# A gated MLP after the last norm: GpSimd's passes go to VectorE, sixteen products move ahead, and down adds into y at once

## The chip, the cores and the metric

The kernel runs on one core of a Trainium2 chip. The metric is the device time of one execution in microseconds. Inputs and outputs are float32.

## The reference

One decoder layer on 512 prompt positions and on 8 sequences of 8 new positions (576 tokens together). The change touches its second half alone:

```python
def conv_ffn(hn, prev_g, w_gate, w_up, conv_w, conv_b, w_down):
    g = hn @ w_gate                     # (T, 2048) @ (2048, 5504)
    u = hn @ w_up
    gp = jnp.concatenate([prev_g.astype(g.dtype), g], axis=1)
    gc = conv_b + sum(conv_w[j] * gp[:, j:j + T] for j in range(CONV_W))
    return (jax.nn.silu(gc) * u) @ w_down, gp[:, T:]
...
    h = x + jnp.concatenate([oa.reshape(B, T, -1), ob.reshape(B, T, -1)], axis=-1) @ w_out
    f, new_g = conv_ffn(rms_norm(h, g_ffn), prev_g, w_gate, w_up, conv_w, conv_b, w_down)
    return h + f, new_rows + (new_g,)
```

## The kernel before

Everything is held transposed: features on the 128 partitions, the 576 tokens along the free dimension in two halves of 288. A float32 product is made of three reduced-precision (float32r) matmuls: each operand is split into a high part (`upper`, a cast on ScalarE, L1571) and a low part (`lower`, a subtraction, L1576), and `multiply` (L1579) runs high x high, high x low and low x high into one PSUM bank. One product of a gate tile is 8 blocks of 128 features times 3, or 24 matmuls of 128x128 by 128x288.

The stages that matter, in order:

- **w_out** (L1657, 16 steps). Each step adds a product to h, squares it on ScalarE (`square`, L1591) and sums the squares on GpSimd (L1595). The first half of h is normalised between the steps (`half0`).
- **Tile 0** (L1752 to L1814). The four weight blocks of tile 0 are multiplied with the first half of h, 4 products, two for gate and two for up. Then the second half is normalised (`norm`, L1767; `normed_h`, L1783 and L1787), and the sums and differences of the halves' blocks are made and split (`tsub`, `thigh`, `tlow`, L1784 to L1797). Then come the other 4 products, and tile 0's convolution and gating.
- **Gate and up, tiles 1 to 42** (L1887). A tile is 128 columns of w_gate and of w_up. The 2x2 block product (gate/up by two halves of the features, times two halves of the features by two halves of the tokens) is made with 7 products in place of 8 (Winograd's form of Strassen's scheme): products 1 and 2 take the blocks a11 and a12 as they are, the others take sums. `ORDER` is 1, 5, 6, 3, 7, 2, 4, and three PSUM banks hold running sums: products 1, 6, 7 and 4 go one after the other into bank "a", 5 and 3 into "b", 2 into "c". Between two products into one bank the running sum is read: ScalarE copies it (`p1s`, `p5s`, `u2s`, L1899 to L1903), or VectorE adds it to a copy. Operands are made three products ahead (`ahead`, L1872; `operand`, L1836): VectorE makes the sums (L1841 to L1850), ScalarE the high parts, and the low parts of products 7, 2 and 4 are GpSimd's, the others VectorE's. The four blocks of the next tile are loaded into 4 buffers (`wr`) as they come free; `wu` and `wl` have 4 buffers each. `conv` (L1728) is one pass on ScalarE, two on VectorE and a silu on ScalarE; `gated` (L1737) multiplies on GpSimd and stores the result to DRAM (`adr`).
- **Down** (L2035). Seven groups q of six row tiles (the last has seven), and four column groups g: 28 items of 7 products, each for two column tiles s, 126 matmuls an item. Weights are 128x768 passes. ScalarE copies products 1, 5 and 6 into snapshots, VectorE adds a snapshot to the bank, and GpSimd adds that to `ht`, which holds y (L2057 to L2065). The activations of the next q (`Acts`) are loaded from `adr`, and eleven passes of 128x864 on VectorE and seven on ScalarE make their sums and parts; they run in the item g = 3 for the most part, when the buffers of the present q come free.
- Outputs are transposed and stored (L2017).

Every load and store named here is issued by SyncE, in one queue. Each engine's instructions run in an order that the framework fixes when it builds the kernel, by a simulated schedule over the program order; buffers are reused only when their readers are done.

Of the kernel before, what the change touches and what calls it, by code (L numbers as in the profile page):

```python
# [48 lines left out]
    0, 1024, 2048, 3072, 3080, 4104, 4360, 4616, 5640, 5704)  # L49
NLATE = 5  # L50
CT = 3


@with_exitstack
def tile_hymba_step(
# [1680 lines left out]

    def gated(j, u):  # L1737

        G.tensor_mul(u[:, :TP], gc[:, :TP], u[:, :TP])
        us = u[:, TP:TP + 56].rearrange("p (b t) -> p b t", t=8)  # L1740
        G.tensor_mul(us, gc[:, TP + 2:TP + 72].rearrange("p (b t) -> p b t", t=10)[:, :, 0:8], us)
        G.tensor_mul(u[:, TP + 56:NT], gc[:, TP + 72:TP + 80], u[:, TP + 56:NT])
        S.dma_start(adr[j], u)

    def blocks(j):
# [3 lines left out]
    V.memset(gx[:, 0:2], 0.0)  # L1749
    states(0)  # L1750

    w0 = {}  # L1752
    for name, at in blocks(0).items():
        t = wload(*at)
        h = upper(t, 1024)
        w0[name] = (h, lower(t, h, 1024, G if name[1] == "2" else V))
    first = [(psum_g(), keep) for keep in (wb.tile([P, HALF], F32, name="sq", bufs=2), ua[:, HALF:])]
    for m, (acc, keep) in enumerate(first):
        multiply(acc, rows8(w0[f"a{m + 1}1"], (hi11, lo11)), True)
        A.copy(keep, acc)  # L1760
    for m, (acc, _) in enumerate(first):
        multiply(acc, rows8(w0[f"a{m + 1}2"], (hi21, lo21)), False)
    A.copy(gx[:, 2:2 + HALF], first[0][0])
    A.copy(ua[:, :HALF], first[1][0])


    for _ in norm(ssum[1], sq1):  # L1767
        pass

    def tsub(dst, x, y):  # L1770
        for k in (0, 4):
# [10 lines left out]
    for o in range(8):  # L1782
        normed_h(o, 1)  # L1783
    tsub(x11, x12, x11)  # L1784
    thigh(hi1, x11)
    for o in range(8, 16):
        normed_h(o, 1)  # L1787
    tlow(lo1, x11, hi1)
    thigh(hi22, x22)
    tsub(x12, x22, x12)  # L1790
    tlow(lo22, x22, hi22)
    thigh(hi3, x12)
    tsub(x22, x22, x11)
    tlow(lo3, x12, hi3, G)
    thigh(hi2, x22)
    tsub(x21, x21, x22)
    tlow(lo2, x22, hi2)  # L1797

    second = [psum_g() for _ in range(2)]
    for m, acc in enumerate(second):  # L1800
        multiply(acc, rows8(w0[f"a{m + 1}1"], (hi1, lo1)), True)
    for m, acc in enumerate(second):
        multiply(acc, rows8(w0[f"a{m + 1}2"], (hi22, lo22)), False)

    gate_half(1, second[0], first[0][1])
    V.tensor_add(ua[:, HALF:], second[1], first[1][1])
# [6 lines left out]
    conv(0)  # L1813
    gated(0, ua)  # L1814

    xops = {1: (hi11, lo11), 5: (hi1, lo1), 6: (hi2, lo2), 3: (hi22, lo22), 7: (hi3, lo3), 2: (hi21, lo21), 4: (hi4, lo4)}
    ORDER = (1, 5, 6, 3, 7, 2, 4)
    BANK = {1: "a", 6: "a", 7: "a", 4: "a", 5: "b", 3: "b", 2: "c"}

    class Weights:  # L1820


        def __init__(self, n, srcs, odd=False):
            self.n, self.m, self.srcs, self.odd = n, n + 256 * odd, srcs, odd
            self.b, self.ready, self.made = {}, {}, 0

        def load(self, name):
            self.b[name] = wload(*self.srcs[name])

        def make(self, n):  # L1830

            while self.made < n:
                self.operand(ORDER[self.made])
                self.made += 1

        def operand(self, i):  # L1836
            b, n, m = self.b, self.n, self.n
            x = b
# [12 lines left out]
            if i in (5, 3, 2, 4):  # L1851
                m = self.m
            src = {1: x["a11"], 5: s0, 6: s1, 3: s0, 7: s1, 2: x.get("a12"), 4: x.get("a22")}[i]
            h = upper(src, m)
            self.ready[i] = (h, lower(src, h, m, G if i in (7, 2, 4) else V))

    items = [Weights(1024, blocks(j)) for j in range(1, NF)]
    NQ = 7
    for q in range(NQ):
        for g in range(4):  # L1860
            srcs = {}
            for m in range(2):
# [7 lines left out]
            items.append(Weights(CT * 256, srcs, q == NQ - 1))  # L1870

    def ahead(at, place, most=7):  # L1872

        n = place + 4
        items[at].make(min(n, 7))
        if at + 1 < len(items):
            for name in {1: ("a11", "a21"), 2: ("a12",), 3: ("a22",)}.get(place, ()):
                items[at + 1].load(name)
        if n > 7 and at + 1 < len(items):
            items[at + 1].make(min(n - 7, most))  # L1880

    for name in ("a11", "a21", "a12", "a22"):
        items[0].load(name)
    items[0].make(3)


    for j in range(1, NF):  # L1887
        w = items[j - 1]
        u = ub if j % 2 else ua
        states(j)  # L1890
        acc = {}
        for place, i in enumerate(ORDER):
            bank = BANK[i]
            if bank not in acc:
                acc[bank] = psum_g() if bank == "a" else psum_s()[:, :HALF]
            d = acc[bank]
            multiply(d, rows8(w.ready.pop(i), xops[i]), i in (1, 5, 2))
            if i == 1:
                A.copy(p1s, d)  # L1899
            elif i == 5:  # L1900
                A.copy(p5s, d)
            elif i == 6:
                A.copy(u2s, d)  # L1903
            elif i == 3:
                gate_half(1, d, u2s)
            elif i == 7:
                V.tensor_add(u[:, HALF:], d, p5s)
            elif i == 2:
                gate_half(0, d, p1s)
                conv(j)  # L1910
            elif i == 4:
                A.copy(u[:, :HALF], d)
            ahead(j - 1, place, 7 if j < NF - 1 else 1)
        gated(j, u)


# [6 lines left out]
    snaps = [[yb.tile([P, HALF], F32, name=f"{n}{s}") for s in range(2)] for n in ("p1s", "p5s", "u2s")]  # L1923
    items[NF - 1].make(3)

    def places(t, n):
        t = t.rearrange("p k t -> p (k t)")
# [107 lines left out]
    for q in range(NQ):  # L2035
        acts[q].finish()
        for g in range(4):
            at = NF - 1 + q * 4 + g
            w = items[at]
            acc = {}  # L2040
            for place, i in enumerate(ORDER):
# [1 line left out]
                h, l = w.ready.pop(i)  # L2043
                xh, xl = acts[q].ops[i]
                for s in range(2):
                    p1s, p5s, u2s = [x[s] for x in snaps]
                    if (bank, s) not in acc:
                        acc[bank, s] = psum_g() if bank == "a" else psum_s()[:, :HALF]
                    d = acc[bank, s]
# [18 lines left out]
                ahead(at, place)  # L2068
# [87 lines left out]
```

## Time and profile before

| | |
|---|---|
| time, median of 3 runs | 3038.9 us (3037.58 to 3039.65) |
| the profiled execution | 3047.65 us, its span 3045.9 us |
| TensorE (PE) busy | 2791.2 us, 92%, 19887 matmuls |
| VectorE (DVE) busy | 1948.2 us, 64% |
| ScalarE (ACT) busy | 1446.8 us, 47% |
| GpSimd (POOL) busy | 1334.2 us, 44% |
| mean granted TensorE clock | 0.968 |

Matmuls overlap, so a busy TensorE is one that has a matmul in flight, not one at its peak; the number of matmuls in a stretch says more. PEld is the loading of weights into TensorE, which runs beside the matmuls. The granted clock is 1 at full speed (2.4 GHz) and 0.5 at the lower level (1.2 GHz). Times in rows are microseconds from the start of the span.

### The profile page before, as it was taken

How to read it: one execution, taken by the hardware profiler on the slowest of the kernel's cores; microseconds unless marked ns; L12 is line 12 of the kernel's file. 1: busy time of each engine (PE TensorE's matmuls, PEld its weight loads, DVE VectorE, ACT ScalarE, POOL GpSimd, SP SyncE). 2: the span in 40 equal slices, each digit the busy share in tenths (PEclk: the TensorE clock that was granted, in tenths of full speed). 3: DMA queues.
4: the chain of work that ended last, by engine and by line, in shares of the span. 5: the costliest groups of instructions: out<-in, count | busy, mean ns of one | idle time of the engine just before them, and what ended most of it. 6: DMA issues, size and time to landing. Idle time of an engine off the chain costs nothing.

```text
span 3045.9 us, 53074 instructions
## 1 busy us (share of the span) xinstructions
PE 2791.2 (92%) x19887; PEld 2657.9 (87%) x19887; DVE 1948.2 (64%) x3168; ACT 1446.8 (47%) x2639; POOL 1334.2 (44%) x1119
## 2 busy tenths in 40 slices
PE   2999999999999999986999999999999988888898
PEld 2999899999898887866999999999999978888898
DVE  2668679555537665647666555665556677777775
ACT  2455643655655566643444433444334444444443
POOL 0233224424553233353544554445444556565565
PEclk7999999999999999987999999999999989999999
DMA  3423343436647898782333333333333443333323
GB/s 76 145 69 97 101 110 96 111 90 179 163 143 222 276 281 276 237 242 69 95 96 96 108 109 102 96 99 112 103 102 95 125 165 105 98 107 97 96 91 111
DMA packets 509713, 395.53 MB, mean 130 GB/s; under 512 B 40901, under 2 KB 451655, under 8 KB 508943
## 3 DMA queue, kind: packets, MB, share of 16 engines
q1 hardware_dynamic: 506046, 381.39, 42.6%
q0 software_dynamic: 3408, 10.75, 1.2%
q8 instruction: 156, 2.56, 0.4%
q14 instruction: 103, 0.84, 0.1%
HBM read 344.20 MB, written 47.59 MB: 129 GB/s over the span
## 4 chain that ended last, share of the span: by engine, by line
DVE 14%; PE 11%; issue 8%; POOL 7%; DMA 7%; ACT 3%; SPq 0%; ACTq 0%; POOLq 0%; DVEq 0%
POOL wl L1576 7%; DMA wr<-in_w_up_dram 5%; DVE wl L1576 4%; ACT wu L1571 3%; PE pgemm L1583 2%; PE pgemm L1584 2%; DVE x L1734 2%; PE pgemm L1586 2%; DMA wr<-in_w_down_dram 2%; DVE x L1841 2%; DVE x L1842 2%; PE pone L1583 2%; PE pone L1584 1%; DVE x L1850 1%; PE pone L1586 1%
## 5 line engine op out<-in xcount | busy, mean ns | idle before, releaser
L171 PE MATMUL pgemm<-xl,wh 128*128 128x288 f32 (+1 forms) x1696 | 512.0, 302 | 52.6 <-DVE xl L304 52.6
L170 PE MATMUL pgemm<-xh,wh 128*128 128x288 f32 (+1 forms) x1824 | 551.4, 304 | 4.6 <-DVE rawT L1339 2.1
L172 PE MATMUL pgemm<-xh,wl 128*128 128x288 f32 (+1 forms) x1824 | 550.2, 302 | 0.7 <-DVE wl L151 0.7
L1571 ACT CAST wu<-x 128x1024 fp32r<-128x1024 f32 x168 | 175.6, 1045 | 470.7 <-DVE x L1841 350.3
L171 PEld LDWEIGHTS pgemm<-xl,wh 128*128 128x128 f32 (+1 forms) x1696 | 322.4, 190 | 59.5 <-DVE xl L304 53.8
L1576 POOL TENSOR_TENSOR wl<-wr,wu 128x1024 fp32r<-128x1024 f32 (+1 forms) x142 | 362.8, 2573 | 12.8 <-ACT wu L1571 12.8
L170 PEld LDWEIGHTS pgemm<-xh,wh 128*128 128x128 f32 (+1 forms) x1824 | 346.0, 190 | 13.8 <-DVE rawT L1339 2.4
L172 PEld LDWEIGHTS pgemm<-xh,wl 128*128 128x128 f32 (+1 forms) x1824 | 346.2, 190 | 6.6 <-issue 1.0
L1583 PE MATMUL pgemm<-xh,wu 128*128 128x288 f32 x1120 | 314.2, 303 | 36.5 <-DVE p5s L2064 17.1
L1583 PE MATMUL pgemm<-hi,wu 128*128 128x288 f32 x784 | 221.0, 306 | 54.2 <-ACT x L1899 43.8
L151 POOL TENSOR_TENSOR wl<-wraw,wh 128x1024 fp32r<-128x1024 f32 (+1 forms) x51 | 122.5, 2402 | 333.6 <-ACT wh L150 331.5
L1571 ACT CAST wu<-wr 128x1024 fp32r<-128x1024 f32 (+1 forms) x230 | 219.9, 978 | 82.3 <-DMA wr<-in_w_gate_dram 35.1
L1583 PEld LDWEIGHTS pgemm<-xh,wu 128*128 128x128 f32 x1120 | 217.2, 194 | 41.5 <-DVE p5s L2064 15.1
L1584 PE MATMUL pone<-xl,wu 128*128 128x288 f32 x816 | 220.8, 295 | 0.0
L1584 PE MATMUL pgemm<-lo,wu 128*128 128x288 f32 x760 | 208.4, 299 | 4.3 <-DVE lo L1780 4.3
L1583 PEld LDWEIGHTS pgemm<-hi,wu 128*128 128x128 f32 x784 | 149.8, 191 | 64.3 <-ACT x L1899 53.1
L1841 DVE TENSOR_TENSOR x<-wr 128x1024 f32<-128x1024 f32 x42 | 53.9, 1284 | 234.4 <-DMA wr<-in_w_up_dram 214.4
L1576 DVE TENSOR_TENSOR wl<-wr,wu 128x1024 fp32r<-128x1024 f32 (+1 forms) x88 | 162.2, 1843 | 64.3 <-ACT wu L1571 64.3
L198 POOL TENSOR_TENSOR svl<-vraw,svh 128x512 fp32r<-128x512 f32 x80 | 110.6, 1397 | 207.1 <-ACT svh L195 116.1
L1571 ACT CAST wu<-sum 128x768 fp32r<-128x768 f32 (+1 forms) x112 | 95.3, 851 | 205.4 <-DVE sum L1841 137.0
L1586 PE MATMUL pgemm<-xh,wl 128*128 128x288 f32 x1120 | 183.8, 299 | 1.6 <-POOL wl L1576 1.1
L1584 PE MATMUL pgemm<-xl,wu 128*128 128x288 f32 x640 | 178.0, 302 | 0.0
(630 smaller groups left out, 8008.2 us busy)
## 6 DMA issues: line engine op xcount, KB each, us to landing
wraw<-in_w_in_dram SPq DMA_DIRECT2D x88, 512.0 KB
wr<-in_w_gate_dram SPq DMA_DIRECT2D x86, 512.0 KB
wr<-in_w_up_dram SPq DMA_DIRECT2D x86, 512.0 KB
wr<-in_w_down_dram SPq DMA_DIRECT2D x112, 384.0 KB
kraw<-in_cache_fox_k_dram SPq DMA_DIRECT2D x128, 256.0 KB
vraw<-in_cache_fox_v_dram SPq DMA_DIRECT2D x128, 256.0 KB
wraw<-in_w_out_dram SPq DMA_DIRECT2D x32, 512.0 KB
dkraw<-in_cache_dsa_k_dram SPq DMA_DIRECT2D x64, 128.0 KB
```

The costliest lines, as they stand in the source:

```text
L151: (G if share[0] and not u else V).tensor_sub(l[:, :k, :m], raw[:, :k, :m], f(h)[:, :k, :m])
L170: T.matmul(acc[:m, :], h[:, j, :m], xh[:, c], start=kt == 0, stop=False)
L171: T.matmul(acc[:m, :], h[:, j, :m], xl[:, c], start=False, stop=False)
L172: T.matmul(acc[:m, :], l[:, j, :m], xh[:, c], start=False, stop=kt == nk - 1)
L198: lo.tensor_sub(l, src, f(h))
L1571: A.copy(h[:, :n], t[:, :n])
L1576: eng.tensor_sub(l[:, :n], t[:, :n], f(h)[:, :n])
L1583: T.matmul(acc, wh, xh, start=start and k == 0, stop=False, skip_group_check=not start)
L1584: T.matmul(acc, wh, xl, start=False, stop=False, skip_group_check=not start)
L1586: T.matmul(acc, wl, xh, start=False, stop=k == len(rows) - 1, skip_group_check=not start)
L1734: V.scalar_tensor_tensor(gc, gx[:, i:i + m], cw[:, i, j:j + 1], gc, op0=OP.mult, op1=OP.add)
L1841: V.tensor_add(s0[:, :n], x["a21"][:, :n], x["a22"][:, :n])
```

## The change

All GpSimd passes of the MLP become VectorE passes: the sums of squares, the low parts, and the gating products (the small copies of the last rows, L1708 and L1709, stay). Tile 0 loses its own code and becomes an ordinary tile. For the first eight tiles (`NPRE`) products 1 and 2 are made ahead of the loop, while the second half of h is normalised and split in steps between them (`half1`); their partial sums go through DRAM (`pdr`), and the loop runs the other five products (`LATER`) and adds the loaded sums. The blocks a11 and a12 of these tiles are loaded and split twice. `ahead` makes one operand after each product, in one list over all tiles and items. In down each running sum is added from its bank to y by VectorE; the snapshots, ScalarE's copies and GpSimd's adds are gone.

```diff
-    def lower(t, h, n, eng=V):
+    def lower(t, h, n):
         l = wq.tile([P, 1024], F32R, name="wl", bufs=4)
-        eng.tensor_sub(l[:, :n], t[:, :n], f(h)[:, :n])
+        V.tensor_sub(l[:, :n], t[:, :n], f(h)[:, :n])
...
-            G.tensor_add(ssum[half], ssum[half], sq)
+            V.tensor_add(ssum[half], ssum[half], sq)
...
-        G.tensor_mul(u[:, :TP], gc[:, :TP], u[:, :TP])
+        V.tensor_mul(u[:, :TP], gc[:, :TP], u[:, :TP])
...
+    pdr = dr.tile([NPRE, 2, P, HALF], F32, name="pdr")
+    early = []
+
+    def prepare(j):
+        if j < NPRE:
+            ts = [wload(*blocks(j)[n]) for n in ("a11", "a12")]
+            hs = [upper(t, 1024) for t in ts]
+            early.append([(h, lower(t, h, 1024)) for t, h in zip(ts, hs)])
+
+    def products(j):
+        acc = psum_g()
+        for i, (w, x) in enumerate(zip(early.pop(0), ((hi11, lo11), (hi21, lo21)))):
+            multiply(acc, rows8(w, x), i == 0)
+            keep = wb.tile([P, HALF], F32, name="sq", bufs=2)
+            A.copy(keep, acc)
+            S.dma_start(pdr[j, i], keep)
...
+    def half1():
+
+        yield from norm(ssum[1], sq1)
+        for o in range(8):
+            normed_h(o, 1)
+        yield
+        tsub(x11, x12, x11)
+        thigh(hi1, x11)
+        yield
+        tlow(lo1, x11, hi1)
+        yield
+        for o in range(8, 16):
+            normed_h(o, 1)
+        thigh(hi22, x22)
+        yield
+        tlow(lo22, x22, hi22)
+        tsub(x12, x22, x12)
+        thigh(hi3, x12)
+        yield
+        tsub(x22, x22, x11)
+        thigh(hi2, x22)
+        tlow(lo3, x12, hi3)
+        yield
+        tlow(lo2, x22, hi2)
+        tsub(x21, x21, x22)
+        yield
+
+    steps = half1()
+    next(steps)
+    prepare(0)
+    for j in range(NPRE):
+        prepare(j + 1)
+        products(j)
+        next(steps, None)
...
+    LATER = (5, 6, 3, 7, 4)
...
+            self.behind = {7: ("a11", "a21") + (() if 2 in order else ("a12",)), 2: ("a12",), 4: ("a22",)}
...
             h = upper(src, m)
-            self.ready[i] = (h, lower(src, h, m, G if i in (7, 2, 4) else V))
+            self.ready[i] = (h, lower(src, h, m))
+            if self.at + 1 < len(items):
+                items[self.at + 1].load(self.behind.get(i, ()))
...
+        items.append(Weights(1024, blocks(j), LATER if j < NPRE else ORDER))
...
+    def ahead(n=1):
+
+        for _ in range(n):
+            if made[0] < len(todo):
+                w, i = todo[made[0]]
+                w.operand(i)
+                made[0] += 1
+
+    items[0].load(("a11", "a21", "a12", "a22"))
+    ahead(3)
...
+        if pre:
+            p1 = prp.tile([P, HALF], F32, name="p1", bufs=2)
+            S.dma_start(p1, pdr[j, 0])
+            S.dma_start(gx[:, 2:2 + HALF], pdr[j, 1])
...
             if i == 1:
                 A.copy(p1s, d)
-            elif i == 5:
-                A.copy(p5s, d)
-            elif i == 6:
-                A.copy(u2s, d)
+            elif i in (5, 6):
+                s = p5s if i == 5 else u2s
+                if pre:
+                    V.tensor_add(s, d, p1)
+                else:
+                    A.copy(s, d)
             elif i == 3:
                 gate_half(1, d, u2s)
+                if pre:
+                    conv(j)
...
-                    if i in (1, 5, 6):
-                        A.copy({1: p1s, 5: p5s, 6: u2s}[i], d)
-                        continue
-                    t, o, n = {3: (u2s, o1, 1), 7: (p5s, o2, 1), 2: (p1s, o1, 0), 4: (None, o2, 0)}[i]
-                    y = ht[:, o, HV[n]]
-                    if t is None:
+
+                    for o, n in {1: ((o1, 0),), 5: ((o2, 1),), 6: ((o1, 1),), 3: ((o1, 1),), 7: ((o2, 1),),
+                                 2: ((o1, 0),), 4: ((o2, 0),)}[i]:
+                        y = ht[:, o, HV[n]]
                         V.tensor_add(y, d, y)
-                    else:
-                        V.tensor_add(t, d, t)
-                        G.tensor_add(y, t, y)
```

## Rows read from the trace of the kernel before

**Rows 1.** Windows by stage: us, busy (instructions) by engine, clock, DMA share, GB/s.

```profile
1395.83:1411.50 15.67, 15.65 (x107) 15.55 (x107) 4.60 (x2) 2.04 (x5) 5.27 (x2) 0.87 0.22 68
1411.50:1458.48 46.98, 24.46 (x150) 23.29 (x150) 41.85 (x63) 17.15 (x18) 12.92 (x4) 0.75 0.00 0
1458.48:2448.21 989.73, 942.91 (x7021) 931.61 (x7022) 595.44 (x626) 410.25 (x559) 480.36 (x336) 1.00 0.37 106
2448.21:2485.00 36.79, 24.06 (x128) 22.28 (x129) 34.45 (x35) 14.84 (x22) 18.02 (x12) 0.73 0.57 200
2485.00:3014.00 529.00, 477.89 (x3413) 466.67 (x3412) 394.53 (x494) 234.10 (x383) 320.79 (x234) 0.97 0.32 102
```

**Rows 2.** Timeline of one gate tile: start, us, engine, instruction, idle before and releaser.

```profile
2003.98 0.19 PEld L1583 LDWEIGHTS pgemm<-hi,wu 128*128 128x128 f32 x1 [1.36 <-ACT x L1899]
2027.59 0.19 PEld L1583 LDWEIGHTS pgemm<-hi,wu 128*128 128x128 f32 x1 [1.31 <-ACT x L1899]
...
2026.19 1.05 ACT L1571 CAST wu<-x 128x1024 fp32r<-128x1024 f32 x1 [1.43 <-DVE x L1846]
...
2020.36 1.22 DVE L1841 TENSOR_TENSOR x<-wr 128x1024 f32<-128x1024 f32 x1 [5.91 <-DMA wr<-in_w_up_dram]
...
2010.60 5.73 POOL L1576 TENSOR_TENSOR wl<-wr,wu 128x1024 fp32r<-128x1024 f32 x2
...
2016.35 0.37 SPq L1565 DMA_DIRECT2D wr<-in_w_up_dram  x1
```

**Rows 3.** TensorE's waits in the gate stage: us in total, times, longest.

```profile
PE pgemm L1583 <- ACT x L1899: 41.6, 37, 1.4
```

**Rows 4.** Waits between the halves of h: us in total, times, longest.

```profile
PE pgemm L1583 <- ACT hi L1776: 9.9, 1, 9.9
...
PE pgemm L1584 <- DVE lo L1780: 4.3, 1, 4.3
```

**Rows 5.** Window of one q of down (columns as in the first group).

```profile
2695.76:2777.21 81.45, 70.86 (x504) 68.64 (x504) 59.66 (x76) 35.75 (x59) 46.87 (x36) 0.98 0.31 99
```

**Rows 6.** TensorE's waits in down: us in total, times, longest.

```profile
PE pgemm L1583 <- DVE p5s L2064: 19.6, 8, 3.1
PE pgemm L1583 <- DVE ht L2062: 12.4, 10, 2.0
```

**Rows 7.** VectorE's timeline in down, at two places of one q.

```profile
2615.25 0.44 DVE L2064 TENSOR_TENSOR u2s<-pone,u2s 128x288 f32<-128x288 f32 x1
2615.62 0.81 DVE L2064 TENSOR_TENSOR p1s<-pone,p1s 128x288 f32<-128x288 f32 x2
...
2645.73 0.96 DVE L1846 TENSOR_TENSOR sum<-wr,sum 128x768 f32<-128x768 f32 x1
2646.61 0.95 DVE L1576 TENSOR_TENSOR wl<-sum,wu 128x768 fp32r<-128x768 f32 x1
```

**Rows 8.** VectorE's groups by form in down: busy us, mean ns, idle before.

```profile
L1576 DVE TENSOR_TENSOR wl<-wr,wu 128x768 fp32r<-128x768 f32 x23 | 36.5, 1589 | 10.6 <-ACT wu L1571 10.6
...
L1957 DVE TENSOR_TENSOR tt<-lo,tt 128x864 f32<-128x864 f32 x5 | 5.2, 1047 | 0.0
```

**Rows 9.** VectorE's groups by form between the halves of h.

```profile
L1772 DVE TENSOR_TENSOR x<-x,x 128x1152 f32<-128x1152 f32 x8 | 10.6, 1349 | 0.0
...
L1627 DVE SCALAR_TENSOR_TENSOR x<-x,g,rb 128x288 f32<-128x288 f32 x16 | 7.0, 513 | 2.0 <-ACT rb L1622 2.0
```

**Rows 10.** Window of w_out (columns as in the first group).

```profile
1300.00:1396.00 96.00, 75.36 (x470) 64.71 (x470) 53.18 (x89) 46.83 (x72) 47.37 (x38) 0.88 0.78 223
```

**Rows 11.** VectorE's timeline in one gate tile.

```profile
2026.02 1.22 DVE L1576 TENSOR_TENSOR wl<-x,wu 128x1024 fp32r<-128x1024 f32 x1
2027.16 0.83 DVE L1734 SCALAR_TENSOR_TENSOR x<-gx,cw,x 128x592 f32<-128x592 f32 x1
2027.90 1.22 DVE L1576 TENSOR_TENSOR wl<-x,wu 128x1024 fp32r<-128x1024 f32 x1
```

**Rows 12.** GpSimd's costliest group by form in the gate stage.

```profile
L1576 POOL TENSOR_TENSOR wl<-wr,wu 128x1024 fp32r<-128x1024 f32 x78 | 220.8, 2852 | 0.0
```

More of the change, by code (lines that the diff above doesn't have):

```diff
@@ L51 @@
 CT = 3
+NPRE = 8
 @with_exitstack
@@ L1737, in gated @@
     def gated(j, u):
-        G.tensor_mul(u[:, :TP], gc[:, :TP], u[:, :TP])
+        V.tensor_mul(u[:, :TP], gc[:, :TP], u[:, :TP])
         us = u[:, TP:TP + 56].rearrange("p (b t) -> p b t", t=8)
-        G.tensor_mul(us, gc[:, TP + 2:TP + 72].rearrange("p (b t) -> p b t", t=10)[:, :, 0:8], us)
-        G.tensor_mul(u[:, TP + 56:NT], gc[:, TP + 72:TP + 80], u[:, TP + 56:NT])
+        V.tensor_mul(us, gc[:, TP + 2:TP + 72].rearrange("p (b t) -> p b t", t=10)[:, :, 0:8], us)
+        V.tensor_mul(u[:, TP + 56:NT], gc[:, TP + 72:TP + 80], u[:, TP + 56:NT])
         S.dma_start(adr[j], u)
@@ L1750, in tile_hymba_step @@
     states(0)
[L1752 to L1768, printed above, removed]
+    pdr = dr.tile([NPRE, 2, P, HALF], F32, name="pdr")
[12 more added lines that the diff above has]
+            S.dma_start(pdr[j, i], keep)
     def tsub(dst, x, y):
@@ L1780, in tlow @@
             eng.tensor_sub(l[:, k:k + 4, :], x[:, k:k + 4, :], f(h)[:, k:k + 4, :])
[L1782 to L1806, printed above, removed]
+    def half1():
[30 more added lines that the diff above has]
+        next(steps, None)
+    for _ in steps:
+        pass
     hb_ctx.close()
@@ L1812, in tile_hymba_step, with __init__, load @@
     wb_ctx.close()
-    conv(0)
-    gated(0, ua)
+    pr_ctx, prp = opened("pr")
     xops = {1: (hi11, lo11), 5: (hi1, lo1), 6: (hi2, lo2), 3: (hi22, lo22), 7: (hi3, lo3), 2: (hi21, lo21), 4: (hi4, lo4)}
     ORDER = (1, 5, 6, 3, 7, 2, 4)
+    LATER = (5, 6, 3, 7, 4)
     BANK = {1: "a", 6: "a", 7: "a", 4: "a", 5: "b", 3: "b", 2: "c"}
     class Weights:
[L1823 to L1834, printed above, removed]
+        def __init__(self, n, srcs, order=ORDER, odd=False):
+            self.n, self.m, self.srcs, self.order, self.odd = n, n + 256 * odd, srcs, order, odd
+            self.b, self.ready, self.at = {}, {}, len(items)
+            self.behind = {7: ("a11", "a21") + (() if 2 in order else ("a12",)), 2: ("a12",), 4: ("a22",)}
+        def load(self, names):
+            for name in names:
+                self.b[name] = wload(*self.srcs[name])
         def operand(self, i):
-            b, n, m = self.b, self.n, self.n
-            x = b
+            x, n, m = self.b, self.n, self.n
             s0, s1 = sums
@@ L1852, in operand @@
                 m = self.m
-            src = {1: x["a11"], 5: s0, 6: s1, 3: s0, 7: s1, 2: x.get("a12"), 4: x.get("a22")}[i]
+            src = {1: x["a11"], 5: s0, 6: s1, 3: s0, 7: s1, 2: x["a12"], 4: x["a22"]}[i]
             h = upper(src, m)
-            self.ready[i] = (h, lower(src, h, m, G if i in (7, 2, 4) else V))
-    items = [Weights(1024, blocks(j)) for j in range(1, NF)]
+            self.ready[i] = (h, lower(src, h, m))
+            if self.at + 1 < len(items):
+                items[self.at + 1].load(self.behind.get(i, ()))
+    items = []
+    for j in range(NF):
+        items.append(Weights(1024, blocks(j), LATER if j < NPRE else ORDER))
     NQ = 7
@@ L1869, in tile_hymba_step @@
                     srcs[f"a{m + 1}{k + 1}"] = at
[L1870 to L1888, printed above, removed]
-        u = ub if j % 2 else ua
-        states(j)
+            items.append(Weights(CT * 256, srcs, odd=q == NQ - 1))
+    todo = [(w, i) for w in items for i in w.order]
+    gate_todo = sum(len(w.order) for w in items[:NF])
+    made = [0]
+    def ahead(n=1):
[6 more added lines that the diff above has]
+    ahead(3)
+    for j in range(NF):
+        w = items[j]
+        pre = j < NPRE
+        u = ub if j % 2 else ua
+        if j:
+            states(j)
+        if pre:
+            p1 = prp.tile([P, HALF], F32, name="p1", bufs=2)
+            S.dma_start(p1, pdr[j, 0])
+            S.dma_start(gx[:, 2:2 + HALF], pdr[j, 1])
         acc = {}
-        for place, i in enumerate(ORDER):
+        for i in w.order:
             bank = BANK[i]
-            if bank not in acc:
+            start = bank not in acc
+            if start:
                 acc[bank] = psum_g() if bank == "a" else psum_s()[:, :HALF]
             d = acc[bank]
-            multiply(d, rows8(w.ready.pop(i), xops[i]), i in (1, 5, 2))
+            multiply(d, rows8(w.ready.pop(i), xops[i]), start)
             if i == 1:
                 A.copy(p1s, d)
-            elif i == 5:
-                A.copy(p5s, d)
-            elif i == 6:
-                A.copy(u2s, d)
+            elif i in (5, 6):
[4 more added lines that the diff above has]
+                    A.copy(s, d)
             elif i == 3:
                 gate_half(1, d, u2s)
+                if pre:
+                    conv(j)
             elif i == 7:
@@ L1910, in tile_hymba_step @@
                 conv(j)
-            elif i == 4:
+            elif pre:
+                V.tensor_add(u[:, :HALF], d, p1)
+            else:
                 A.copy(u[:, :HALF], d)
-            ahead(j - 1, place, 7 if j < NF - 1 else 1)
+            if made[0] <= gate_todo:
+                ahead()
         gated(j, u)
@@ L1922, in tile_hymba_step @@
     sums = [yb.tile([P, 1024], F32, name=f"sum{i}") for i in range(2)]
-    snaps = [[yb.tile([P, HALF], F32, name=f"{n}{s}") for s in range(2)] for n in ("p1s", "p5s", "u2s")]
-    items[NF - 1].make(3)
+    ahead(2)
     def places(t, n):
@@ L2037, in tile_hymba_step @@
         for g in range(4):
-            at = NF - 1 + q * 4 + g
+            at = NF + q * 4 + g
             w = items[at]
@@ L2045, in tile_hymba_step @@
                 for s in range(2):
-                    p1s, p5s, u2s = [x[s] for x in snaps]
                     if (bank, s) not in acc:
@@ L2055, in tile_hymba_step @@
                     o1, o2 = 2 * g + s, 8 + 2 * g + s
[L2056 to L2061 removed]
+                    for o, n in {1: ((o1, 0),), 5: ((o2, 1),), 6: ((o1, 1),), 3: ((o1, 1),), 7: ((o2, 1),),
+                                 2: ((o1, 0),), 4: ((o2, 0),)}[i]:
+                        y = ht[:, o, HV[n]]
                         V.tensor_add(y, d, y)
[L2063 to L2065 removed]
                 if g == 3:
                     slots.extend(acts[q].ops.pop(i))
[L2068 removed]
+                ahead()
                 if q + 1 < NQ:
@@ L2080, in tile_hymba_step @@
     yb_ctx.close()
+    pr_ctx.close()
     fn_ctx.close()
```

## The prediction

> **What bounds the kernel now.** I read the page first (TensorE is busy for most of the span, VectorE for two thirds, GpSimd for under half), then the windows by stage, then in each stage the waits of TensorE, one period in the timeline, and the mean durations by form. The reader should see that TensorE sets the pace everywhere and that each stage loses its time differently.
>
> - Gate/up stage, the third window, 989.7 us [rows 1]. One tile takes 23.61 us from one stall's end to the next (the two PEld rows, 2003.98 to 2027.59), 1.31 us of it idle [rows 2]. So a product of 24 matmuls costs (23.61 - 1.31)/7 = 3.186 us. The waits give the stall to the copy of product 1 out of its bank, 41.6 us in 37 tiles [rows 3]. Followed back in [rows 2]: the copy on ScalarE stands behind a cast that waits for VectorE (L1846); VectorE had sat 5.91 us until a block of w_up landed; SyncE issued that load at 2016.35, when GpSimd ended two subtractions that hold the buffer (2010.60 + 5.73). The late engine is GpSimd.
> - Between the halves of h, the second window [rows 1]: of 46.98 us TensorE works 24.5, at a mean granted clock of 0.75 (1 is 2.4 GHz, 0.5 is 1.2). Its longest waits are for hi and lo of the second half [rows 4], while VectorE works 41.9 us.
> - Down, the last window, 529 us, some 26 items [rows 1]. Four items, one value of q, take 81.45 us [rows 5], and 504 matmuls at 3.186/24 us are 66.9. TensorE waits there for VectorE's adds [rows 6] while VectorE is busy 59.7 of 81.45 us, part of it stretched: subtractions of one size take 0.95 us beside an idle GpSimd [rows 7] and 1.59 on average in the group that runs beside it [rows 8].
>
> **The change, part by part.**
>
> *Square sums to VectorE.* Some 29 adds of 128x288, near 0.5 us each by the nearest row, L1627 with 513 ns [rows 9], so 13 us of VectorE in the stretch of w_out, where it is busy 53.2 of 96 us [rows 10]. They fit its idle time; without that cover they cost 13 us. I take 0, bounds -5 to +7 (gain: the norm no longer waits for GpSimd's slower sums).
>
> *Tile 0 becomes an ordinary tile.* 8 products become 7: from 1395.83 to 2448.21, the first three windows, which is 1052.4 us [rows 1], 302 products become 301, and 301 x 3.186 = 959. So 93 us of that stretch can at most be had. What will be lost of it again:
>
>  (a) The 16 early products are 51 us of TensorE. VectorE must do beside them 18 passes of 128x1152 at 1.27 us (duration 1.35, they overlap by 0.08) [rows 9], two of which come from GpSimd, 7.0 us of scaling [rows 9], about 3 of newton, and 16 weight subtractions at 1.14 us (start to start) [rows 11]: 51 us too. The weight loads are queued on SyncE behind stores of partial products, which wait for ScalarE's copies, which wait for TensorE; whoever is late delays the next tile's operands. Loss taken: 10 us, bounds 2 to 35.
>  (b) The hand-over: hi4, lo4 are in the 18 passes, but the first three operands of item 0 need 6 more passes, 7 us, and casts. 8 us, bounds 3 to 15.
>  (c) Eight tiles of 5 products, 15.9 us each. VectorE has 9 weight passes (10.3), convolution 1.5 (0.74 each) [rows 11], five or so adds of a half (1.9), gating and state about 1.3: 15.0 us, 94%. And the block a22 is loaded only after operand 4, with three products (9.6 us) until the next item's first one; the landing of 4 us (issued 2016.35, VectorE released 2020.36) [rows 2], two sums, a cast and a subtraction need about 10. So each tile waits a little: 2.5 us, bounds 0.5 to 5; eight tiles, 20 us.
>  (d) Thirty-five tiles of 7 products: GpSimd's 2.85 us subtraction [rows 12] becomes 1.14 on VectorE, which has 11 x 1.14 + 1.5 + 1.5 + 1.3 = 16.8 of 22.3 us. The block of w_up is free 4 to 5 us sooner, against a stall of 1.31. The gating products wait for ScalarE's silu with VectorE's other passes behind them, so not all goes: 0.3 us left, bounds 0 to 1.2; 10 us.
>
>  After: 959 + 10 + 8 + 20 + 10 = 1007, gain 45, bounds 88 (all lower bounds) and -20 (all upper ones: 959 + 35 + 15 + 40 + 42 = 1091 would be -39; they hardly meet, so I stop at half of the last two).
>
> *Hand-over to down*, the fourth window [rows 1]. Passes stretched by GpSimd shrink, but product 1 now needs y itself loaded. +3, bounds -4 to +8.
>
> *Down.* Three copies on ScalarE, eight VectorE adds and six GpSimd adds per item become 14 VectorE adds from PSUM; three weight subtractions come over from GpSimd. By start-to-start times [rows 7]: 11 x 0.88 + 14 x 0.37 = 14.9 us per item, under 16.7 of TensorE. But the eleven passes that make the next activations (1.05 us [rows 8], 0.97 less the same overlap) fall on one item of four, whose buffers come free then: 14.9 + 10.7 = 25.6 us. New wait: TensorE's next product into a bank waits for VectorE's add of the last one, and the adds stand in line with passes of about 1 us; the tightest is from product 4 to the next item's product 1, with one half-product (1.2 us) between. I give it 0.5 us an item: 3 x 17.2 + 25.6 = 77.2 per q against 81.45. Gain 4.2 x 6.5 = 27 us. Bounds: VectorE never idle, 4 x 14.9 + 10.7 = 70.3, gain 72; no overlap between passes (16.75 an item, 11.6 for the activations, 1.5 us a hand-over) 84.6, loss 21.
>
> The Trainium skill, "Perfetto Trace Analysis", section "Optimizing Scalar/DVE Operations", speaks against this part: a saturated VectorE should give work to ScalarE or even GpSimd, with the reserve that GpSimd and VectorE share a read port. By that advice down would not gain and the sum would be the second rival's; the trace supports the reserve (1.59 against 0.95 us [rows 7, 8]) and leaves open whether 70 of 77 us is saturation.
>
> **The sum.** 0 + 45 + 3 + 27 = 75 us off the profiled execution (3047.65, that is 1.75 outside its span of 3045.9): 2972.7. The median of the runs is 8.75 below that execution, so 2964.
>
> **Rivals.**
>
> 1. *TensorE alone sets the pace.* The lower bounds of (a) to (d) give 88, and down runs at 68 us per q: 6.5 x 13.4 = 87. With 3: 2861. For it: VectorE's mean load is below TensorE's in every part. Against: in (a) and (c) the margin is nil, and in down one item of four is over.
> 2. *VectorE is the bound of down*, so nothing is gained there: 45 + 3, 2991. For it: 19.6 us per item when durations are added without overlap, activations included. Against: most of today's VectorE passes there are stretched, and that ends.
> 3. *The early products do not fill the gap*: loads behind stores and passes in one queue stretch them to 75 us, loss (a) 35: 75 - 25 = 50, 2989. This is the case in which this part doesn't do what it says. For it: 51 us of VectorE in 51 us. Against: the transfers run nearly idle there (DMA share 0.00 in the second window [rows 1]).
> 4. *The bank hand-overs make it slower.* Every bank waits for VectorE's queue now. If eight hand-overs an item are late by 0.6 us each, an item takes 16.7 + 4.8 + 2.7 = 24.2 us against 20.36 now: 26 x 3.84 = 100 lost, 3038.9 - 48 + 100 = 3091. It decides once an item passes 20.36 + 48/26 = 22.2 us. For it: TensorE already waits on VectorE's adds [rows 6]. Against: all but one hand-over have 3.5 us of other products between, and passes are 1 us.
>
> **How the numbers follow.** Forecast 0.53 (its own range 2925 to 2995), rival 1 0.10, rival 2 0.16, rival 3 0.12, rival 4 0.09. Predicted 2964. The range 2900 to 3010 leaves out most of rival 1 (0.08), rival 4 (0.09) and little else. A difference of 0.2%, 6 us, is about what this kernel's runs can tell from no change. Faster: the first four cases less 0.02 of their tails, 0.89; within 0.2%: that and 0.01 of rival 4, 0.03; slower: 0.08.
>
> **What would show it.** (a) No TensorE gap over 5 us between the last product of w_out and the gate stage, clock near 1; (c) tiles of 17 to 19 us for the first eight; (d) a period of 22.3 to 23 us and no wait on the copy of product 1, subtractions all near 1.22 us; down: a period per q of 74 to 80 us, VectorE busy over 85%. Wrong would be: VectorE idle for a load where I have it working, a stall at each bank hand-over, or an early stage over 70 us.

## The result, and the profile after

The changed kernel takes 2956.2 us (median of 4 runs, 2950.9 to 2966.5) against 3039.3: a ratio of 0.9732, 95% interval 0.9705 to 0.9758. A second set of five runs beside the experiments gave 2960.0 us and 0.9724 (0.9707 to 0.9740). The forecast was 2964.

First the windows of the changed kernel by stage, and one q of down (us, busy time and instructions of PE, PEld, DVE, ACT and POOL, then clock, DMA share, GB/s). They answer to [rows 1, 5, 10].

```profile
1300.00:1394.50 94.50, 75.91 (x484) 65.62 (x482) 60.86 (x123) 47.03 (x73) 11.24 (x8) 0.89 0.81 235
1394.50:1454.57 60.07, 56.80 (x398) 55.24 (x398) 52.98 (x70) 29.85 (x40) 0.00 (x0) 0.95 0.54 154
1454.57:1619.77 165.20, 147.23 (x1036) 145.12 (x1037) 127.64 (x177) 61.86 (x69) 4.67 (x16) 0.95 0.47 134
1619.77:2391.90 772.13, 772.13 (x5819) 771.64 (x5817) 570.43 (x723) 353.26 (x459) 47.96 (x70) 1.00 0.40 113
2391.90:2430.00 38.10, 25.56 (x143) 24.08 (x143) 37.12 (x52) 14.16 (x19) 0.00 (x0) 0.78 0.55 193
...
2629.51:2706.07 76.56, 70.14 (x504) 68.60 (x505) 70.13 (x112) 28.67 (x35) 0.00 (x0) 0.98 0.34 106
```

Three things stand there. In the long gate window TensorE is busy for 772.13 of 772.13 us: 5819 matmuls at 132.7 ns, no stall left. In the window before it, which holds the eight short tiles, it is idle for 18 us. In down one q takes 76.56 us where it took 81.45, and VectorE is busy for 70.13 of them, 92%.

Next the waits of the changed kernel: TensorE's over the short tiles, then the main one in down (us in total, times, longest). In the long gate window TensorE has none; the wait of [rows 3] is gone.

```profile
PE pone L1584 <- ACT wu L1572: 15.1, 6, 3.7
PE pgemm L1584 <- DVE gx L1702: 2.4, 1, 2.4
...
PE pgemm L1584 <- DVE ht L2084: 34.4, 21, 4.2
```

And one short tile of the changed kernel in its timeline, the chain behind one of those waits (VectorE, SyncE, VectorE, ScalarE, TensorE).

```profile
1539.77 1.22 DVE L1577 TENSOR_TENSOR wl<-wr,wu 128x1024 fp32r<-128x1024 f32 x1
...
1541.02 0.37 SPq L1566 DMA_DIRECT2D wr<-in_w_up_dram  x1
...
1546.55 1.23 DVE L1848 TENSOR_TENSOR x<-wr 128x1024 f32<-128x1024 f32 x1 [2.01 <-DMA wr<-in_w_up_dram]
...
1547.87 1.04 ACT L1572 CAST wu<-x 128x1024 fp32r<-128x1024 f32 x1 [4.19 <-DVE x L1848]
...
1548.96 0.61 PE L1584 MATMUL pone<-hi,wu 128*128 128x288 f32 x1 [3.70 <-ACT wu L1572]
```

Read it downwards: the subtraction for operand 4 ends at 1540.99 and frees the buffer; the load of the next tile's a22 goes out 0.03 us later and takes 5.5 us; the sum, the cast, and TensorE has waited 3.70 us.

### The profile page after: what moved, and what is told of

Read it like the earlier page. It is cut to its first block, busy times and chain, and to the rows that moved or that the text cites. A ratio compares the mean times of both kernels' runs of the same rounds, so it can differ in the third digit from the quotient of the medians.

```text
span 2964.4 us, 52612 instructions
## 1 busy us (share of the span) xinstructions
PE 2773.7 (94%) x19863; PEld 2653.4 (90%) x19863; DVE 2135.4 (72%) x3732; ACT 1414.1 (48%) x2458; POOL 501.6 (17%) x579
## 4 chain that ended last, share of the span: by engine, by line
PE 50%; DVE 9%; DMA 7%; issue 2%; ACT 1%; SPq 1%; POOL 0%; DVEq 0%; ACTq 0%; POOLq 0%
PE pgemm L1584 8%; PE pgemm L1585 8%; PE pgemm L1587 7%; PE pone L1584 6%; PE pone L1585 5%; PE pone L1587 5%; DVE wl L1577 3%; DMA wr<-in_w_up_dram 2%; PE pone L1394 2%; DMA wr<-in_w_down_dram 1%; DVE ht L2084 1%; PE pgemm L171 1%; PE pgemm L172 1%; PE pgemm L173 1%; PE pout L1464 1%
## 5 line engine op out<-in xcount | busy, mean ns | idle before, releaser
L1577 DVE TENSOR_TENSOR wl<-wr,wu 128x1024 fp32r<-128x1024 f32 (+1 forms) x229 | 258.3, 1133 | 120.9 <-ACT wu L1572 116.5
L1709 POOL COPY cn<-gx 128x2 f32<-128x2 f32 x43 | 45.8, 1065 | 1013.5 <-DVE gx L1725 1013.5
L1577 DVE TENSOR_TENSOR wl<-x,wu 128x1024 fp32r<-128x1024 f32 x172 | 209.1, 1219 | 1.6 <-ACT wu L1572 0.5
L1585 PE MATMUL pone<-xl,wu 128*128 128x288 f32 x768 | 208.9, 297 | 0.0
L1585 PE MATMUL pgemm<-xl,wu 128*128 128x288 f32 x680 | 185.8, 298 | 0.0
L152 POOL TENSOR_TENSOR wl<-wraw,wh 128x1024 fp32r<-128x1024 f32 (+1 forms) x51 | 122.0, 2392 | 338.9 <-ACT wh L151 336.9
L151 ACT CAST wh<-wraw 128x1024 fp32r<-128x1024 f32 (+1 forms) x122 | 127.1, 1042 | 97.5 <-PE pgemm L172 89.9
L1584 PE MATMUL pone<-hi,wu 128*128 128x288 f32 x536 | 150.9, 304 | 19.9 <-ACT wu L1572 15.8
```

The lines of the kernel that those rows point to most:

```text
L151: A.copy(h[:, :k, :m], raw[:, :k, :m])
L152: (G if share[0] and not u else V).tensor_sub(l[:, :k, :m], raw[:, :k, :m], f(h)[:, :k, :m])
L1577: V.tensor_sub(l[:, :n], t[:, :n], f(h)[:, :n])
L1584: T.matmul(acc, wh, xh, start=start and k == 0, stop=False, skip_group_check=not start)
L1585: T.matmul(acc, wh, xl, start=False, stop=False, skip_group_check=not start)
L1709: G.tensor_copy(c[:, j % CN, 0:2], gx[:, TP:TP + 2])
```

## The experiments

Every ratio is to the kernel before, measured on the same chip in the same series. The changed kernel ran in one of the four series (e11) and has 0.9724 there, 0.9707 to 0.9740; runs of different series are compared by these ratios, and 0.001 is 3 us.

### Which engine makes the low parts

**e1.** The changed kernel with three low parts of the gate stage back on GpSimd.

```diff
-            self.ready[i] = (h, lower(src, h, m))
+            self.ready[i] = (h, lower(src, h, m, G if i in (7, 2, 4) and self.n == 1024 else V))
```

> The changed kernel, but in the gate stage the low parts of products 7, 2 and 4 are GpSimd's again (down keeps them on VectorE). Theory A (the stall of 1.31 us a tile came from GpSimd holding the weight buffers): the tiles from the ninth on go back from 22.3 us to 23.3 to 23.8 us, with the wait on the copy of product 1 back, and the eight short tiles from 20 us to 22 or more; in all 45 to 65 us slower than the changed kernel. Theory B (the new order of loads and operands removed the stall, the engine does not matter): within 10 us of the changed kernel.

2987.5 us, 0.9816 (0.9799 to 0.9833): 28 us slower than the changed kernel. Its window of 25 ordinary tiles, and two stalls of TensorE in it, one tile apart:

```profile
1652.68:2237.14 584.46, 564.23 (x4207) 558.20 (x4207) 339.10 (x451) 243.91 (x332) 209.70 (x125) 1.00 0.37 104
```

```profile
1652.68 0.40 PE L1584 MATMUL pgemm<-hi,wu 128*128 128x288 f32 x1 [0.89 <-ACT x L1918]
...
1676.12 0.41 PE L1584 MATMUL pgemm<-hi,wu 128*128 128x288 f32 x1 [0.92 <-ACT x L1918]
```

584.46/25 = 23.4 us a tile, with the wait on the copy of product 1 back: theory A on the mechanism. Its total was too large, because the short tiles went the other way: 18.5 us (1473.07 to 1491.55) in place of 19 to 20, where theory A had said 22 or more. A likely reason is that operand 4's pass, on GpSimd, no longer stands in VectorE's line; no run tests it.

**e7.** The converse: the kernel before with that one line changed.

```diff
-            self.ready[i] = (h, lower(src, h, m, G if i in (7, 2, 4) else V))
+            self.ready[i] = (h, lower(src, h, m))
```

> The kernel before with one line changed: the low parts of products 7, 2 and 4 on VectorE, in gate and down. Theory A (this move alone gives most of the change): tiles at 22.3 us from 23.6, 45 to 55 us, and down 5 to 30 us faster: 2955 to 2990. Theory B (the new order of loads and the early products were needed as well): tiles stay above 23 us, less than 25 us faster than before.

2947.9 us, 0.9681 (0.9665 to 0.9697). Theory A, and more than it asked: one line gives 97 us, more than the whole change. From its windows:

```profile
2473.42:2547.71 74.29, 69.44 (x505) 68.32 (x505) 67.52 (x87) 36.02 (x60) 30.21 (x24) 0.98 0.32 101
1452.82:1489.95 37.13, 36.49 (x273) 36.25 (x273) 26.47 (x32) 17.66 (x23) 10.44 (x10) 1.00 0.47 130
1489.95:2386.00 896.05, 895.77 (x6748) 895.27 (x6748) 633.75 (x721) 411.67 (x537) 154.24 (x200) 1.00 0.39 112
```

Gate runs without a stall here too, with the old loop and the old loads, and one q of down takes 74.29 us, less than the changed kernel's 76.56. The gain lies in both stages: by the profiled runs, the last silu of the gate stage comes 62 us earlier than before (2385.9 for 2448.1), and from there to the end it takes 562 us in place of 598.

**e12.** Why did GpSimd's passes cost that: by holding a weight buffer, or by stretching VectorE's passes? The kernel before keeps all its GpSimd passes and gets a fifth buffer, in room that is free once the second half is normalised.

```diff
-        t = wq.tile([P, 1024], F32, name="wr", bufs=4)
+        t = pool.tile([P, 1024], F32, name="w22") if pool else wq.tile([P, 1024], F32, name="wr", bufs=4)
...
+            own = name == "a22" and self.at % 2 and self.at < NF - 1
+            self.b[name] = wload(*self.srcs[name], pool=prp if own else None)
...
-            for name in {1: ("a11", "a21"), 2: ("a12",), 3: ("a22",)}.get(place, ()):
+            for name in ({1: ("a11", "a21"), 2: ("a12", "a22")} if at < NF - 2 else
+                         {1: ("a11", "a21"), 2: ("a12",), 3: ("a22",)}).get(place, ()):
```

> The kernel before, GpSimd passes and all, with a fifth weight buffer in the gate stage: every other a22 block has its own, and no a22 load waits for GpSimd's pass on operand 4. Theory A (GpSimd held the buffer, so the load came late, so TensorE stalled): VectorE's wait of 5.9 us for w_up goes to under 2 us and the tiles to 22.3 to 22.6 us, 35 to 50 us faster than before. Theory B (GpSimd stretching VectorE's passes made the stall): the load is early but the tiles stay at 23.2 to 23.7 us, under 15 us faster.

2983.6 us, 0.9820 (0.9795 to 0.9844), 55 us faster than before. Its window of the gate stage, VectorE's main wait and its most stretched group:

```profile
1500.00:2380.00 880.00, 880.00 (x6643) 879.74 (x6643) 586.96 (x590) 409.13 (x524) 438.18 (x316) 1.00 0.39 111
```

```profile
DVE x L1847 <- DMA wr<-in_w_up_dram: 239.1, 35, 10.3
```

```profile
L1848 DVE TENSOR_TENSOR x<-x,wr 128x1024 f32<-128x1024 f32 x40 | 83.6, 2089 | 1.9
```

GpSimd is busy half the time (438 of 880 us) and stretches the passes of this group from 1.22 to 2.09 us, and TensorE has no stall at all. So in the gate stage of the kernel before it was the held buffer: theory A. The edit also asks for the a22 block one product earlier, which the free buffer makes possible. Down is as before (597 us from the last silu to the end, 598 before), so the 36 us that e7 gained there are not explained by this run; whether GpSimd's low parts cost them by a held buffer or by stretching is not shown. One part of its expectation failed: VectorE's wait for w_up is not under 2 us but 6.8 (239.1/35). That wait is now slack; VectorE comes to it early.

**e9.** GpSimd busy beside the gate stage but holding nothing: e7 with 126 added subtractions (added work; the outputs are the same).

```diff
         gated(j, u)
+        for _ in range(3):
+            G.tensor_sub(scratch, f(hi11)[:, 0:3, :], f(lo11)[:, 0:3, :])
```

> The kernel before with the low parts on VectorE, and beside the gate stage 126 subtractions of 128x864 on GpSimd that read two tiles nobody writes and whose result nobody reads (added work, the outputs are the same): GpSimd is busy but holds no weight buffer. They depend on nothing, so they run in one row from the start of the gate stage, some 300 us. Theory A (in the kernel before the tile's stall came from weight buffers held by GpSimd): tiles stay at 22.3 us beside them, within 10 us of the kernel without them. Theory B (it came from GpSimd stretching VectorE's passes): tiles beside them take 23.3 us or more, 13 of them, so 13 us or more in all, and later ones 22.3.

3095.0 us, 1.0181 (1.0161 to 1.0201), some 150 us slower than e7 by the ratios. A window beside the added work and one after it, and VectorE's group beside it:

```profile
1600.00:1700.00 100.00, 77.35 (x515) 76.16 (x514) 85.37 (x55) 30.00 (x41) 89.55 (x44) 0.86 0.28 79
2000.00:2100.00 100.00, 100.00 (x756) 100.00 (x755) 68.55 (x78) 44.27 (x59) 20.64 (x24) 1.00 0.40 113
```

```profile
L1576 DVE TENSOR_TENSOR wl<-x,wu 128x1024 fp32r<-128x1024 f32 x42 | 87.6, 2087 | 0.0
```

515 matmuls in 100 us against 756: a tile takes 100 x 168/515 = 32.6 us. The added passes, stretched themselves, lasted for 450 us (1448 to 1900) and not 300. Neither theory had the size; theory A is wrong as a general statement, and theory B's 13 us were ten times too few. A GpSimd busy 90% of the time stalls the stage with no weight buffer in its hands, by stretching VectorE's passes (GpSimd's own products are not late: VectorE waits for GpSimd for 3.9 us in 340); 3 of the 10 us a tile are the lower granted clock of that window (0.86: 515 matmuls in 77.35 us busy are 150 ns each, against 132). At about half, GpSimd did not stall it (e12).

### The early products

**e2, e3.** No tile, or four, made ahead in place of eight.

```diff
-NPRE = 8
+NPRE = 0
```

> The changed kernel with no product made ahead (NPRE = 0): every tile has 7 products, and the second half of h is normalised with TensorE idle. Theory A (the early products only move the loss: what they fill, some 30 us between the halves, the eight short tiles give back at 4 us each): within 10 us of the changed kernel, with an idle stretch of 25 to 35 us in TensorE and 22.3 us for every tile. Theory B (filling the gap was worth its 30 us): 25 to 40 us slower.

2966.0 us, 0.9743 (0.9727 to 0.9760). The gap is back, as one row of its timeline shows, and the time hardly moves: theory A.

```profile
1424.99 0.61 PE L1584 MATMUL pone<-hi,wu 128*128 128x288 f32 x1 [27.51 <-ACT wu L1572]
```

> The changed kernel with four tiles made ahead in place of eight. Theory A: the early stretch has 25 us of products beside about 40 us of VectorE passes, so 10 to 15 us of idle come back, and four short tiles less save 16 us: between 8 us faster and 3 us slower than the changed kernel. Theory B: half the fill is lost, 12 to 20 us slower.

2959.4 us, 0.9724 (0.9707 to 0.9740), the changed kernel's own ratio: theory A. Between none and eight tiles made ahead lies at most 0.2%: what the 16 early products fill (27.5 us of waiting in e2), the short tiles give back (28 us, worked out below).

**e4.** The changed kernel with a fifth buffer for the short tiles, all four loads once product 7's operand is made.

```diff
+            if self.at < NPRE:
+                self.behind = {7: ("a11", "a21", "a12", "a22")}
...
+                own = name == "a22" and self.at % 2 and self.at <= NPRE
+                self.b[name] = wload(*self.srcs[name], pool=prp if own else None)
```

> The changed kernel with one more weight buffer for the first eight tiles: every other a22 block gets its own buffer, so that all four blocks of the next tile are loaded once product 7's operand is made, and none waits for operand 4. Theory A (the short tiles are held by the ring from operand 4 over the load of a22 to the next tile's sums): 16 to 17.5 us a short tile in place of 20, 20 to 28 us faster than the changed kernel. Theory B (VectorE's load of 94% holds them): 19 to 20 us a tile, within 6 us of the changed kernel.

2944.7 us, 0.9676 (0.9660 to 0.9692). TensorE's stalls at the heads of two short tiles, four tiles apart, and their sum over the stretch:

```profile
1463.88 0.40 PE L1584 MATMUL pone<-hi,wu 128*128 128x288 f32 x1 [0.47 <-ACT wu L1572]
...
1530.28 0.40 PE L1584 MATMUL pone<-hi,wu 128*128 128x288 f32 x1 [0.29 <-ACT wu L1572]
```

```profile
PE pone L1584 <- ACT wu L1572: 4.8, 6, 1.7
```

Four tiles in 66.4 us (1463.88 to 1530.28), 16.6 each: theory A, the ring over the a22 buffer. The total, some 15 us by the ratios, is a little under its 20 to 28.

### Down

**e5.** ScalarE copies products 1, 5 and 6; VectorE adds the copies.

```diff
-                        V.tensor_add(y, d, y)
+                    if i in (1, 5, 6):
+                        t = snaps[(1, 5, 6).index(i)][s]
+                        A.copy(t, d)
+                        V.tensor_add(y, t, y)
+                    else:
+                        V.tensor_add(y, d, y)
```

> The changed kernel, but in down ScalarE copies products 1, 5 and 6 out of their banks and VectorE adds the copies to y: as many VectorE adds, with three of seven banks released by ScalarE. Theory A (VectorE's work, 70 us a q, bounds down at about 76.6 us a q): within 1.5 us a q, so within 10 us of the changed kernel. Theory B (TensorE's waits at the bank hand-overs, VectorE's adds standing in line behind passes, are what is lost): 3 to 6 us a q less, 20 to 35 us faster.

2956.5 us, 0.9717 (0.9701 to 0.9733), no difference that these runs can tell. One of its windows of a q: VectorE has the same 70 us.

```profile
2541.26:2615.99 74.73, 69.47 (x504) 68.57 (x504) 70.27 (x112) 36.43 (x59) 0.00 (x0) 0.98 0.34 103
```

Three such windows are 75.05, 74.73 and 78.21 us, 76.0 on average, as in the changed kernel (73.72, 77.59 and 76.56, also 76.0): theory A. Whether ScalarE or VectorE releases these three banks does not matter.

**e6.** The adds of the kernel before: copies on ScalarE, eight adds on VectorE, six on GpSimd.

```diff
-                        V.tensor_add(y, d, y)
+                    if i in (1, 5, 6):
+                        A.copy({1: p1s, 5: p5s, 6: u2s}[i], d)
...
+                            V.tensor_add(t, d, t)
+                            G.tensor_add(y, t, y)
```

> The changed kernel with the adds into y as in the kernel before (ScalarE copies, VectorE adds a snapshot, GpSimd adds to y); the low parts stay on VectorE. VectorE then has 8 adds an item in place of 14, 9 us a q less. Theory A (VectorE's amount of work bounds down, and GpSimd's small adds stretch its passes little): 72 to 75 us a q, 10 to 30 us faster than the changed kernel. Theory B (GpSimd's adds stretch VectorE's passes by more than they relieve it): 78 to 81 us a q, 10 to 30 us slower.

2950.0 us, 0.9692 (0.9676 to 0.9709), 10 us faster than the changed kernel, at the edge of theory A. A window of one q, and the group of VectorE that pays the most:

```profile
2548.65:2623.97 75.32, 68.63 (x505) 67.04 (x505) 67.31 (x87) 36.07 (x60) 28.71 (x24) 1.00 0.31 99
```

```profile
L1849 DVE TENSOR_TENSOR sum<-sum,wr 128x768 f32<-128x768 f32 x19 | 23.9, 1255 | 0.0
```

VectorE has 24 passes less in a q (88 or 87 for 112), worth 9 us, but only 3 us less busy time, since passes beside GpSimd are stretched, in this group from 0.95 to 1.26 us. That is still 1.3 us a q to the good (74.7 on average over three q, against 76.0). The comparison with the changed kernel goes over two series, but e8 against e4, which differ in the same adds, has the same sign and 16 us.

**e8, e10.** Both gains together; and then also the four sums of the next activations on GpSimd.

```diff
                 t = yb.tile([P, CT, HALF], F32, name="tt", bufs=3)
-                V.tensor_sub(t, x, y)
+                G.tensor_sub(t, x, y)
```

> The changed kernel with both of the parts that gained: the fifth weight buffer for the first eight tiles, and down's adds into y as in the kernel before. Theory A (the two losses lie in different stages and add up): 25 to 35 us faster than the changed kernel, 2920 to 2932. Theory B (one of them only moves a wait to the hand-over between the stages): no faster than the better of the two alone, 2942 to 2950.

2926.5 us, 0.9622 (0.9608 to 0.9636): theory A, the gains add up: 15 (e4) and 10 (e6) by the ratios, 31 together, or 34 by the medians of e8 and e11, which ran in one series. It is the fastest kernel here.

> The fifth buffer and down's adds as before, and the four sums of each q's next activations in down on GpSimd in place of VectorE. Theory A (VectorE's amount of work in the item where the activations are made sets down's loss): VectorE has 3.9 us a q less, 1.5 to 4 us a q gained, 10 to 25 us faster than without this. Theory B (GpSimd's slower passes stand in the chain of the activations and stretch VectorE's): 0 to 4 us a q lost, the same or up to 25 us slower.

2956.2 us, 0.9715 (0.9697 to 0.9733), 30 us slower than e8: theory B. One q of e8, then one of e10:

```profile
2447.87:2521.92 74.05, 69.45 (x504) 68.41 (x504) 67.77 (x88) 35.91 (x60) 31.26 (x25) 0.97 0.35 110
```

```profile
2560.71:2640.67 79.96, 71.12 (x504) 69.93 (x504) 70.82 (x84) 35.95 (x60) 40.99 (x28) 0.95 0.33 102
```

Four passes went from VectorE and its busy time rose by 3 us. How much of the loss is this stretching, and how much the later operands, no run tells apart.

**e11.** The changed kernel again.

> The changed kernel once more, unchanged, beside the other three on the same chip, as their measure: 0.973 of the kernel before.

2960.0 us, 0.9724 (0.9707 to 0.9740).

## Why the prediction was right, step by step

- **The stall in gate** was read rightly: GpSimd held the buffer, the load came late, TensorE stalled. e12 removes the hold and keeps every GpSimd pass, and the stall is gone; e1 brings GpSimd back, and so is the stall. Term (d) kept 0.3 us a tile, 10 us in all; measured is 0.
- **The sums of squares** were put at 0; w_out ends 1.3 us earlier (1394.50 for 1395.83), no more than runs differ by.
- **(a), the early stretch**: 51 + 10 us forecast, 60.1 measured.
- **(b) and (c)** were mis-sized against each other. The hand-over cost 0.7 us, not 8: TensorE's wait before 1454.57. The eight short tiles took 19.4 us each on average, not 18.4, as this window of them shows (columns as above):

```profile
1454.57:1609.81 155.24, 137.27 (x962) 135.16 (x962) 117.71 (x164) 55.56 (x61) 4.67 (x16) 0.95 0.48 138
```

  Their 40 products are 127.4 us at 3.186, so 28 us were lost where (c) had 20: 18 idle, and 10 in slower matmuls, with the granted clock at 0.95 on average. The chain from operand 4 over the load was named, but its load was put at 4 us and takes 5.5; the clock had no term. From 1454.57 to the end of gate TensorE has 285 products, 908 us at 3.186, and took 937.3: 29 us lost where (b) to (d) had 38. That (b) came out 7 below its term and (c) 8 above is luck for the sum.
- **The whole stretch from w_out to down**: 60.1 + 937.3 = 997 us, forecast 1007, before 1052. The gain is 55, not 45; the 10 us between are term (d), which was not spent.
- **Down with its hand-over**: from the end of gate to the end of the span 597.7 us before, 572.5 after, 25 gained and 30 forecast. The period of a q was forecast at 77.2 and is 73.7 to 77.6, 76.0 on average; VectorE's work was put at 70.3 us and is 70.1. Three q before took 81.1 on average, so at 5.1 us a q the stretch should have gained 33; the other q and the two ends gained less, and the hand-over window is no shorter (38.1 us with 143 matmuls for 36.8 with 128), where 3 us were forecast. The mechanism is half right: the forecast had one long item of 25.6 us and three of 17.2, and the four items of the q shown above, 126 matmuls each by their starts (a window also counts those that reach into it), are

```profile
2629.51:2651.50 21.99, 19.41 (x126) 18.51 (x127) 20.19 (x31) 7.38 (x9) 0.00 (x0) 0.92 0.26 86
2651.50:2669.75 18.25, 16.92 (x128) 16.72 (x127) 15.32 (x27) 5.65 (x7) 0.00 (x0) 1.00 0.33 105
2669.75:2686.38 16.63, 16.63 (x129) 16.63 (x127) 14.93 (x25) 5.76 (x7) 0.00 (x0) 1.00 0.31 96
2686.38:2706.07 19.69, 17.18 (x128) 16.74 (x127) 19.69 (x32) 9.89 (x12) 0.00 (x0) 1.00 0.45 139
```

  The loss is where VectorE is full (20.19 of 21.99 us, 19.69 of 19.69), but it spreads over two items, and the third runs at TensorE's pace.
- **Rivals.** TensorE alone setting the pace holds in gate from the ninth tile on, not in down. The late bank hand-overs of rival 4 are there, 34 us in 538 (2392 to 2930), but an item costs 19.0 us (76.0/4), far from the deciding 22.2; e5 says that they are the form in which VectorE's load shows, not a cost of their own. Rival 3 was half right in substance: the early part gives nothing (e2), yet for another reason, since the products did fill the gap and the short tiles gave it back.
- **What the forecast did not see**: the change is not the sum of three gains. One line of it gives 97 us (e7), the early products about 0 (e2, e3), and down's adds lose 10 (e6). The sums of squares, the gating products and tile 0's loss of its own code were not timed alone. The Trainium skill, "Perfetto Trace Analysis", section "Optimizing Scalar/DVE Operations", says that giving some of a saturated VectorE's work to GpSimd may make sense, and warns that it might not help, because the two share a read port. Both show here: the six small adds an item on GpSimd gained 10 us (e6), the four sums a q lost 30 (e10).
- **Slips in its sums**, none of which moved the forecast: the lower bounds of (a) to (d) add up to a gain of 84, not 88 (rival 1 is then 2865); with half of the last two upper bounds the gain is +2, not -20; and rival 3's early stretch of 75 us goes with a loss of 24 in (a), while its loss of 35 would be a stretch of 86.

What stays open: why e7 has 2 or 3 us less than e6, which is within what these runs can tell; by which of the two ways GpSimd's low parts cost 36 us in down; and how busy GpSimd may be beside the gate stage before its stretching alone stalls TensorE, which lies somewhere between half (e12) and nine tenths (e9), with passes of other sizes.

## What to carry to other kernels

A slow engine off the critical path can set the pace through a buffer that it holds: follow the late load back to the instruction that freed its buffer, and try one more buffer as well as a faster engine (e12 and e7 both removed the stall). Work made ahead to fill a gap must be priced with what it leaves behind: here the short tiles met a ring of buffers that the full ones did not. When a change bundles parts, time each alone; two of these three were worth nothing or less, and leaving one out while mending another gave 34 us more.

## What the runs showed of the hardware

In these runs a small VectorE copy that starts under a GpSimd pass ends only when that pass ends. Here is the copy of 16 columns at L1701, first in the kernel before with the GpSimd pass that runs beside it, then its mean over the gate stage:

```profile
2006.57 1.29 DVE L1701 COPY gx<-sts 128x16 f32<-128x16 f32 x1
2005.19 2.64 POOL L1739 TENSOR_TENSOR x<-x 128x512 f32<-128x512 f32 x1 [12.38 <-ACT x L1735]
```

```profile
L1701 DVE COPY gx<-sts 128x16 f32<-128x16 f32 x39 | 49.1, 1260 | 0.0
```

The pass ends at 2007.83 and the copy at 2007.86. In the gate stages of the kernel before and of e12, 80 of these 81 copies began under a GpSimd pass, and each of the 80 ended 0.03 to 0.04 us after it. Without such a pass the copy takes 0.17 us, as in the changed kernel (first row). In e9, with GpSimd busy for 90% of the time, it takes no longer where it begins just before a GpSimd pass (the other two rows): 12 of its 14 copies there began under none, and took 0.16 to 0.17 us.

```profile
1549.94 0.17 DVE L1702 COPY gx<-sts 128x16 f32<-128x16 f32 x1
...
1622.46 0.16 DVE L1701 COPY gx<-sts 128x16 f32<-128x16 f32 x1
1622.48 1.29 POOL L1739 TENSOR_TENSOR x<-x 128x512 f32<-128x512 f32 x1 [2.91 <-ACT x L1735]
```

So for this copy the price is what is left of the GpSimd pass, whatever GpSimd's busy share. Not every VectorE pass pays: the adds at L1722, which read a PSUM bank, took 0.446 us in e9 beside the busy GpSimd (below) and 0.451 later in the same run, with GpSimd busy for a fifth of the time, while the 128x1024 passes, whose operands all lie in SBUF, took 2.09 us and later 1.22.

```profile
L1722 DVE TENSOR_TENSOR gx<-pone,x 128x288 f32<-128x288 f32 x10 | 4.5, 446 | 0.0
```
